# A state space model stepped by two tokens: states of odd tokens alone, even outputs by maps of their own

## Chip, cores and metric

One core of a Trainium2 chip. The metric is the device time of one launch in microseconds (us): the median of several runs, lower is better. The kernel before takes 2031.93 us.

## The reference

The program is a three-branch layer with a mixture of experts, followed by two layers of another kind; one batch, 256 tokens, width 1024, float32 throughout. The change touches the first branch, a diagonal state space model of 32 groups with 16 channels and 64 complex states each:

```python
def s5_branch(u, lam_re, lam_im, log_dt, b_re, b_im, c_re, c_im, d_skip, w_glu):
    uf = u.astype(F32).reshape(bsz, seq, SSM_GROUPS, SSM_GROUP)
    lam_bar = jnp.exp(lam * dt)
    b_bar = ((lam_bar - 1.0) / lam)[..., None] * b
    bu = jnp.einsum('bsgh,gph->bsgp', uf.astype(jnp.complex64), b_bar)
    _, states = lax.associative_scan(_ssm_combine, (a, bu), axis=1)   # s_t = lam_bar * s_(t-1) + bu_t
    y = jnp.real(jnp.einsum('bsgp,ghp->bsgh', states, c))
    y = y + d_skip * uf
    y = jax.nn.gelu(y)
    y = y * jax.nn.sigmoid(y @ w_glu)
```

Beside it run a sparse attention over 64 chosen keys (8 heads, with an index score that chooses them) and an attention over a memory of 256 rows (4 heads). Gates merge the three, an output projection adds them to x, and the experts and the two further layers follow.

## The kernel before

Activations lie as 128 channels (partitions) by 256 tokens. Dense weights come in units of 1 MB, two **pieces** of 128x1024 each (`slot`, two buffers). ScalarE (ACT) rounds a piece (`parts`, L223), VectorE (DVE) subtracts to get the rest (`parts`, L224), and TensorE (PE) multiplies in three passes (L232 to L234), 24 passes of 256 columns a piece. Three buffers of `parts` let ACT and DVE be three pieces ahead of PE. For one projection the tokens are the stationary side (L1210, 12 passes of 512 columns a piece).

The state space model stands in `class Ssm`. Set-up makes the decay and the maps `bl` (input to state, real and imaginary) by DVE and by transposes on PE (L545). For each of 16 pairs of groups (four chunks `c` of four, `j`) `chunk` does this: two float32 products of 32 rows by 128 columns over 256 tokens into one bank `ss` (L580); two multiplications on DVE by tables of cosine and sine (L587, L588), which turn the state's frame so that its decay is real; two additions on GpSimd (POOL; L589, L590); two scans along the tokens on DVE (L593); a multiplication back on DVE (L597) and one on POOL (L598); four float32 products of 128 rows by 32 columns over 256 tokens, all into the same 32 rows of the chunk's bank `yb` (L600). One float32 matmul shows in the profile as two records. `gelu` then ends a chunk. Banks of PSUM: two `dn`, four `at`, two `ss`. The two attentions (`attend`) run between chunks 0, 1, 2 and 3, and gate projections fill in.

The scheduler of the framework writes the order of the instructions on each engine when the program is built; at run time an engine takes them in that order and stops at the first that has to wait. The experts (`moe`) load 192 units of 1 MB in the order of SP's queue; the first nine (`ahead`) are issued one behind each of the last nine units of this layer's dense weights.

Of the kernel before, what the change touches and what calls it, by code (L numbers as in the profile page):

```python
# [8 lines left out]
F32 = mybir.dt.float32  # L9
# [136 lines left out]
class Ctx:  # L146
# [352 lines left out]

class Ssm:  # L500


    def __init__(self, K, pool, V):
        self.K, self.pool, self.V = K, pool, V
        nc = K.nc
        S = Small(K, pool, [128, 16], "s16", 28)
        ec = pool.tile([128, 16], F32, name="ec")
        nc.vector.memset(ec, math.e)
        dt, r = S.t(), pool.tile([128, 16], F32, name="decay")
# [4 lines left out]
        nc.vector.tensor_scalar(turn, th, 1 / (2 * math.pi), None, op0=OP.mult)  # L514
        nc.gpsimd.tensor_tensor(r, ec, lr, op=OP.pow)
        self.r = r
        sn, cs = sincos(S, K, th)
        a = S.ts(S.tt(r, cs, OP.mult), -1.0, OP.add)
        b = S.tt(r, sn, OP.mult)
        den = S.t()  # L520
        nc.vector.reciprocal(den, S.tt(S.tt(V["lre"], V["lre"], OP.mult), S.tt(V["lim"], V["lim"], OP.mult), OP.add))
        fr = S.tt(S.tt(S.tt(a, V["lre"], OP.mult), S.tt(b, V["lim"], OP.mult), OP.add), den, OP.mult)
        fi = S.tt(S.tt(S.tt(b, V["lre"], OP.mult), S.tt(a, V["lim"], OP.mult), OP.subtract), den, OP.mult)
# [3 lines left out]
        cd = pool.tile([128, 3, 16, 32], F32, name="cd")  # L527
        nc.scalar.dma_start(cd[:, :2], K.d["ssmc"])
        nc.scalar.mul(cd[:, 2], cd[:, 1], -1.0)
        self.cd = cd  # L530

        self.bl = []
        W = Small(K, pool, [128, 16, 16], "s1", K.n["s1"])
        frb, fib = (t[:, :, None].to_broadcast([128, 16, 16]) for t in (fr, fi))
        for n, (x, y, op) in enumerate(((frb, fib, OP.subtract), (fib, frb, OP.add))):
            p = W.tt(bc[:, 0], x, OP.mult)
            q = W.tt(bc[:, 1], y, OP.mult)
            bd = pool.tile([128, 16, 32], F32, name="bd", tag="s2", bufs=K.n["s2"])
            nc.gpsimd.memset(bd, 0.0)
            for g in range(2):  # L540
                s = slice(64 * g, 64 * g + 64)
                nc.vector.tensor_tensor(bd[s, :, 16 * g:16 * g + 16], p[s], q[s], op=op)
            bk = K.bank("ss")
            for c in range(4):
                nc.tensor.transpose(bk[:, c * 128:(c + 1) * 128],  # L545
                                    bd[:, 4 * c:4 * c + 4].rearrange("p a b -> p (a b)"), K.ident)
            bl = pool.tile([128, 4, 128], F32, name=f"bl{n}")
            nc.vector.tensor_copy(bl.rearrange("p a b -> p (a b)"), bk)
            self.bl.append(bl)
# [3 lines left out]
    def tables(self, c):  # L553

        K, pool, nc, turn = self.K, self.pool, self.K.nc, self.turn
        if self.tt is None:
            self.tt = pool.tile([128, T], F32, name="iota_t")
            nc.gpsimd.iota(self.tt, pattern=[[1, T]], base=0, channel_multiplier=0,
                           allow_small_or_imprecise_dtypes=True)
        tt = self.tt  # L560
        sn = pool.tile([128, 4, T], F32, name="sn", tag="tab", bufs=K.n["tab"])
        cs = pool.tile([128, 4, T], F32, name="cs", tag="tab", bufs=K.n["tab"])
        nc.gpsimd.tensor_tensor(sn, tt[:, None, :].to_broadcast([128, 4, T]),
                                turn[:, 4 * c:4 * c + 4, None].to_broadcast([128, 4, T]), op=OP.mult)
# [7 lines left out]
    def chunk(self, u, c, yb):  # L572

        K, pool, nc = self.K, self.pool, self.K.nc
        for j in range(4):
            i = 4 * c + j
            p = slice(32 * j, 32 * j + 32)
            bk = K.bank("ss")
            for n in range(2):
                nc.tensor.matmul(bk[:, n * T:(n + 1) * T], self.bl[n][p, c], u[p, c], start=n == 0, stop=True,  # L580
                                 skip_group_check=True)
# [1189 lines left out]
```

## Time and profile before

| what | value |
|---|---|
| three runs | 2032.91, 2031.72, 2031.93 us, median 2031.93 us |
| the profiled execution | 2030.49 us, its span 2028.5 us |
| share of the span, PE / DVE / ACT / POOL | 92% / 60% / 40% / 7% |
| mean granted clock of PE | 0.955 |

The span runs from the first to the last instruction; 2.0 us of the execution lie around it. A PE record lasts longer than it holds the engine, since records overlap: the time of one is read from one start to the next. The same holds, by some 0.08 us, on DVE.

### The profile page before, as it was taken

The numbers are of one execution on the slowest core, as the hardware profiler recorded it, in microseconds if no ns is written. First come the engines' busy times: TensorE is split into PE (matmuls) and PEld (weight loads), VectorE is DVE, ScalarE is ACT, GpSimd is POOL, SyncE is SP. The second block draws the span as 40 slices with busy tenths as digits, with TensorE's granted clock in tenths as the row PEclk, the third lists the DMA queues.
The fourth block names the chain that finished last, engine by engine and source line by source line (L and its number), as shares of the span: only waits on it lengthen the run. The fifth ranks groups of instructions, "written<-read, shape, count | busy, mean of one in ns | idle before, by whom it ended". The sixth has DMA issues, their size and how long they took to land.

```text
span 2028.5 us, 33538 instructions
## 1 busy us (share of the span) xinstructions
PE 1857.4 (92%) x14114; PEld 1506.7 (74%) x14114; DVE 1219.7 (60%) x1967; ACT 814.5 (40%) x1273; POOL 147.1 (7%) x110
## 2 busy tenths in 40 slices
PE   7999997876767678999999999999999899999999
PEld 6877896322212224999889998998999888998998
DVE  7898773111101104777597677777877687667775
ACT  6455542000000003544455545444544365445543
POOL 4254201000000001000100000000000100001000
PEclk9999998888887888999999999999999999999999
DMA  5422287999999998655334455554655333455553
GB/s 201 146 98 90 84 332 287 421 421 421 421 421 421 421 421 318 208 188 188 121 127 142 150 188 210 188 186 146 209 185 191 135 130 126 158 176 208 207 184 108
DMA packets 64139, 455.51 MB, mean 225 GB/s; under 512 B 7553, under 2 KB 7841, under 8 KB 9201
## 3 DMA queue, kind: packets, MB, share of 16 engines
q1 hardware_dynamic: 62960, 451.56, 59.7%
q8 instruction: 112, 1.84, 0.4%
q10 hardware_dynamic: 864, 1.41, 0.2%
q0 software_dynamic: 160, 0.35, 0.0%
q14 instruction: 43, 0.34, 0.0%
HBM read 452.25 MB, written 1.05 MB: 223 GB/s over the span
## 4 chain that ended last, share of the span: by engine, by line
PE 55%; DMA 21%; DVE 4%; ACT 2%; issue 1%; SPq 0%; DVEq 0%; ACTq 0%
DMA ahead<-wmoe 9%; PE bk_dn L241 7%; PE bk_ss L241 7%; PE bk_dn L232 5%; PE bk_dn L233 5%; PE bk_dn L234 5%; DMA parts<-wmoe 4%; PE bk_at L233 4%; DMA mraw<-wmoe 4%; PE bk_at L234 4%; PE bk_at L232 4%; PE bk_ss L242 4%; PE bk_dn L242 4%; DMA slot<-wmoe 3%; DVE parts L224 2%; PE bk_dn L1210 2%
## 5 line engine op out<-in xcount | busy, mean ns | idle before, releaser
L224 DVE TENSOR_TENSOR parts<-slot,parts 128x1024 fp32r<-128x1024 f32 x468 | 585.2, 1259 | 197.0 <-ACT parts L223 194.6
L223 ACT CAST parts<-slot 128x1024 fp32r<-128x1024 f32 x468 | 485.5, 1051 | 393.1 <-PE bk_dn L234 183.0
L234 PE MATMUL bk_dn<-hp,parts 128*128 128x256 f32 x976 | 283.0, 290 | 3.2 <-DVE parts L224 3.2
L233 PE MATMUL bk_dn<-hp,parts 128*128 128x256 f32 x976 | 281.6, 289 | 4.3 <-DVE hp L285 4.3
L232 PE MATMUL bk_dn<-hp,parts 128*128 128x256 f32 x976 | 281.1, 288 | 4.0 <-DVE kb L1375 1.8
L241 PE MATMUL bk_dn<-hp,parts 128*128 128x512 f32 x704 | 252.0, 394 | 2.4 <-DVE hp L285 2.4
L241 PE MATMUL bk_ss<-hp,parts 128*128 128x512 f32 x704 | 251.3, 393 | 0.0
L242 PE MATMUL bk_ss<-hp,parts 128*128 128x256 f32 x704 | 198.6, 282 | 0.3 <-DVE parts L224 0.3
L242 PE MATMUL bk_dn<-hp,parts 128*128 128x256 f32 x704 | 198.1, 282 | 0.0
L234 PEld LDWEIGHTS bk_dn<-hp,parts 128*128 128x128 f32 x976 | 188.9, 194 | 11.7 <-issue 6.9
L232 PEld LDWEIGHTS bk_dn<-hp,parts 128*128 128x128 f32 x976 | 188.8, 194 | 11.3 <-issue 6.7
L233 PEld LDWEIGHTS bk_dn<-hp,parts 128*128 128x128 f32 x976 | 188.7, 194 | 10.9 <-DVE hp L285 5.6
L233 PE MATMUL bk_at<-hidp,parts 128*128 128x256 f32 x704 | 195.4, 282 | 0.4
L234 PE MATMUL bk_at<-hidp,parts 128*128 128x256 f32 x704 | 194.9, 282 | 0.0
L232 PE MATMUL bk_at<-hidp,parts 128*128 128x256 f32 x704 | 186.6, 283 | 2.3 <-DVE hidp L350 2.1
L241 PEld LDWEIGHTS bk_dn<-hp,parts 128*128 128x128 f32 x704 | 132.3, 189 | 29.1 <-issue 3.4
L241 PEld LDWEIGHTS bk_ss<-hp,parts 128*128 128x128 f32 x704 | 132.3, 188 | 28.8 <-ACT parts L223 0.8
L1081 DVE TENSOR_TENSOR mhid<-ms,bk_dn 128x512 f32<-128x512 f32 x8 | 5.5, 688 | 223.2 <-PE bk_dn L1074 223.2
L242 PEld LDWEIGHTS bk_dn<-hp,parts 128*128 128x128 f32 x704 | 133.2, 189 | 3.0 <-issue 1.6
L242 PEld LDWEIGHTS bk_ss<-hp,parts 128*128 128x128 f32 x704 | 133.1, 189 | 2.1 <-DVE parts L224 0.6
L233 PEld LDWEIGHTS bk_at<-hidp,parts 128*128 128x128 f32 x704 | 133.6, 190 | 1.0 <-DVE hidp L351 1.0
L232 PEld LDWEIGHTS bk_at<-hidp,parts 128*128 128x128 f32 x704 | 128.8, 190 | 6.8 <-issue 3.0
(437 smaller groups left out, 2975.7 us busy)
## 6 DMA issues: line engine op xcount, KB each, us to landing
slot<-wdense SPq DMA_DIRECT2D x235, 1024.0 KB, 4.9
ahead<-wmoe SPq DMA_DIRECT2D x99, 1024.0 KB, 19.8
mraw<-wmoe SPq DMA_DIRECT2D x40, 1024.0 KB, 19.8
parts<-wmoe SPq DMA_DIRECT2D x31, 1024.0 KB, 19.8
slot<-wmoe SPq DMA_DIRECT2D x22, 1024.0 KB, 19.8
x<-xt SPq DMA_DIRECT2D x2, 512.0 KB, 5.5
memt<-memt SPq DMA_DIRECT2D x1, 1024.0 KB, 12.4
out<-x SPq DMA_DIRECT2D x4, 256.0 KB, 2.5
```

The costliest lines, as they stand in the source:

```text
L223: nc.scalar.copy(hi, raw)
L224: nc.vector.tensor_sub(lo, raw, hi.bitcast(F32))
L232: nc.tensor.matmul(out, whi[:, wsl], h.part(0, k), start=first, stop=False, **kw)
L233: nc.tensor.matmul(out, whi[:, wsl], h.part(1, k), start=False, stop=False, **kw)
L234: nc.tensor.matmul(out, wlo[:, wsl], h.part(0, k), start=False, stop=last, **kw)
L241: nc.tensor.matmul(bank, whi[:, wsl], h.both(k).rearrange("p a t -> p (a t)"), start=first, stop=False, **kw)
L242: nc.tensor.matmul(half(bank, 0), wlo[:, wsl], h.part(0, k), start=False, stop=last, **kw)
L1081: nc.vector.tensor_mul(hid, s, hb[1])
L1210: nc.tensor.matmul(bks[t], h.part(hp, k, slice(t * 128, t * 128 + 128)), w[wp][:, i * 512:(i + 1) * 512], start=k == 0 and n == 0, stop=k ...
```

## The change

The recurrence is stepped by two tokens. With tokens split into even (e) and odd (o), the state at an odd token is `lam_bar^2` times the state at the odd token before, plus a map (`bl[0]`, with `lam_bar` folded in) of the even input and a map (`bl[1]`) of the odd input: 128 states a row in place of 256, so the tables, multiplications, scans and additions are half as long. The output at an odd token comes from its state by the old map (`cd`); the output at an even token comes from the state of the odd token before it by a map with `lam_bar` folded in (`ce`, 127 columns), plus a direct product of its input (`direct`, 128x128). Tokens of a chunk lie apart, even ones first, from `u` (written with the two halves apart) to the last multiplication of `gelu` (which puts them in order again).

Two pairs of groups are done at once: their input products go alternately to two `ss` banks from different rows of the array (`chain`), and the sixteen output products of a chunk go in turn to four different columns of 32 (`together`), all at the chunk's end, into a bank `at`. Set-up makes two more maps `bl`, `direct` (32 products of 32x32) and `ce`. The copies of `bl` and those of `pt` in `attend` that DVE did go to ACT.

```diff
+    def chain(self, issues):
+        m = issues[0]()
+        for f in issues[1:]:
+            with self.tc.issue_after(m.ins):
+                m = f()
...
-        nc.vector.tensor_scalar(turn, th, 1 / (2 * math.pi), None, op0=OP.mult)
+        nc.vector.tensor_scalar(turn, th, 1 / (2 * math.pi), 2.0, op0=OP.mult, op1=OP.mult)
...
+        self.r = pool.tile([128, 16], F32, name="decay")
+        nc.vector.tensor_mul(self.r, r, r)
...
+        gr = S.tt(S.tt(ar, fr, OP.mult), S.tt(ai, fi, OP.mult), OP.subtract)
+        gi = S.tt(S.tt(ar, fi, OP.mult), S.tt(ai, fr, OP.mult), OP.add)
...
+        for m, (x, y) in enumerate(((gr, gi), (fr, fi))):
...
+                bl = pool.tile([128, 4, 128], F32, name=f"bl{m}{n}")
+                nc.scalar.copy(bl.rearrange("p a b -> p (a b)"), bk)
...
+        bk = K.bank("ss")
+        for n in range(2):
+            for i in range(16):
+                p, o = slice(32 * (i % 4), 32 * (i % 4) + 32), n * 128 + i // 4 * 32
+                nc.tensor.matmul(bk[p, o:o + 32], bds[n][:, i], cd[:, n, i], start=n == 0 and i < 4, stop=True,
+                                 skip_group_check=True)
...
+            nc.vector.tensor_sub(self.direct[p, :, 32 * j:32 * j + 32], bk[p, :128].rearrange("p (c m) -> p c m", c=4),
+                                 im[p])
...
+        for n, (x, y, op) in enumerate(((ar, ai, OP.subtract), (ai, ar, OP.add))):
+            t = s2("cm")
+            nc.vector.tensor_mul(ce[:, n], cd[:, 0], x)
+            nc.vector.tensor_mul(t, cd[:, 1], y)
+            nc.vector.tensor_tensor(ce[:, n], ce[:, n], t, op=op)
...
+        hs = []
+        for j in (0, 2):
+            bks = [K.bank("ss") for _ in range(2)]
+            K.chain([into(bk, j + i, n, a) for a in range(2) for n in range(2) for i, bk in enumerate(bks)])
+            h, m = (pool.tile([128, 2, 2, H], F32, name=n, tag="s2", bufs=K.n["s2"]) for n in ("sh", "sm2"))
+            cs, sn = (t[c][:, j:j + 2, None, :].to_broadcast([128, 2, 2, H]) for t in (self.cs, self.sn))
+            for i, bk in enumerate(bks):
+                v = bk[:, :T].rearrange("p (n t) -> p n t", n=2)
+                nc.vector.tensor_mul(h[:, i], v, cs[:, i])
+                nc.vector.tensor_mul(m[:, i], v, sn[:, i])
+            nc.gpsimd.tensor_tensor(h[:, :, 0], h[:, :, 0], m[:, :, 1], op=OP.subtract)
+            nc.gpsimd.tensor_tensor(h[:, :, 1], h[:, :, 1], m[:, :, 0], op=OP.add)
+            for i in range(2):
+                for n in range(2):
+                    nc.vector.tensor_tensor_scan(m[:, i, n], self.r[:, 4 * c + j + i:4 * c + j + i + 1]
+                                                 .to_broadcast([128, H]), h[:, i, n], 0.0, OP.mult, OP.add)
+            for i in range(2):
+                nc.vector.tensor_mul(h[:, i], m[:, i], cs[:, i])
+                nc.gpsimd.tensor_tensor(m[:, i], m[:, i], sn[:, i], op=OP.mult)
+            nc.gpsimd.tensor_tensor(h[:, :, 0], h[:, :, 0], m[:, :, 1], op=OP.add)
+            nc.gpsimd.tensor_tensor(h[:, :, 1], m[:, :, 0], h[:, :, 1], op=OP.subtract)
+            hs += [h[:, 0], h[:, 1]]
+        yb = half(K.bank("at"), 0)
+        nc.tensor.matmul(yb[:, :H], self.direct[:, c], u[:, c, :H], start=True, stop=False, skip_group_check=True)
...
+        K.together([out(j, n, a) for a in (1, 0) for n in range(2) for j in range(4)])
...
+        nc.vector.tensor_mul(g.rearrange("p (k a) -> p a k", a=2), apart(th), apart(y))
...
-        (nc.scalar.copy if i % 4 else nc.vector.tensor_copy)(flat(pt), bk)
+        nc.scalar.copy(flat(pt), bk)
...
+            for i in range(w):
+                nc.vector.tensor_mul(u[:, c + i].rearrange("p (a k) -> p k a", a=2),
+                                     ps[:, i].rearrange("p (k a) -> p k a", a=2),
+                                     N.rb.rearrange("p (k a) -> p k a", a=2))
```

What this does to the order of the instructions is shown at three places; rows of the change have its own line numbers (L625 are the input products, L652 the direct one, L656 the output products, L637 and L638 the multiplications after the input products, L643 the scans, L646 the multiplication back, L231 the subtraction of `parts`, L239 to L241 the passes).

PE before, in chunk 0, among the passes with the tokens stationary (L1210): the four output products of one pair of groups, then the two input products of a later one.

```order
L1210 MATMUL bk_dn<-parts,hp 128x512 x12
L600 MATMUL bk_ss<-p_1055,cd 32x256 x2
L600 MATMUL bk_ss<-p_1056,cd 32x256 x2
L580 MATMUL bk_ss<-u,bl_857 128x256
L580 MATMUL bk_ss<-u,bl_872 128x256
L1210 MATMUL bk_dn<-parts,hp 128x512 x8
```

PE now, 32 passes behind the last of those passes: all outputs of chunk 0.

```order
L848 MATMUL bk_at<-cbase,rs_r 128x128 x8
L652 MATMUL bk_at<-u,direct 128x128
L656 MATMUL bk_at<-sh,ce 32x127
L656 MATMUL bk_at<-sh,cd 32x128 x8
L656 MATMUL bk_at<-sh,ce 32x127 x7
```

What stood in sixteen places of the program as groups of four products of 256 columns stands in four places as groups of seventeen products of 128.

PE now, a little later (chunk 1, its second two pairs of groups; ten passes stand behind these rows and ahead of the next).

```order
L625 MATMUL bk_ss<-u,bl_872 128x128 x2
L625 MATMUL bk_ss<-u,bl_887 128x128 x2
L625 MATMUL bk_ss<-u,bl_902 128x128 x2
L625 MATMUL bk_ss<-u,bl_917 128x128 x2
L239 MATMUL bk_dn<-hp,parts 128x256
```

PE, what follows: the next group of input products (chunk 2), which writes the same two `ss` banks, begins right behind the first scores of the attention; one pass is put inside it.

```order
L81 MATMUL bk_at<-sq,cbase 32x256 x4
L880 LDWEIGHTS identb
L880 MATMUL bk_at<-madd_617,identb 128x512
L880 LDWEIGHTS identb
L880 MATMUL bk_at<-madd_617,identb 128x512
L885 MATMUL bk_at<-kr,qr 128x256 x4
L240 MATMUL bk_dn<-hp,parts 128x256
L241 MATMUL bk_dn<-hp,parts 128x256
L625 MATMUL bk_ss<-u,bl_872 128x128
```

DVE now, what empties the two banks between these two groups: the four multiplications stand between the subtractions of the 26th and the 27th piece.

```order
L231 TENSOR_TENSOR parts<-slot,parts 128x1024
L824 TENSOR_SCALAR madd_617<-ca 128x256
L453 TENSOR_TENSOR sm<-sm 128x256
L822 SCALAR_TENSOR_TENSOR ca<-isc,ca 128x256
L637 TENSOR_TENSOR sh<-bk_ss,cs 128x256
L824 TENSOR_SCALAR madd_620<-ca 128x256
L638 TENSOR_TENSOR sm_1568<-bk_ss,sn 128x256
L637 TENSOR_TENSOR sh<-bk_ss,cs 128x256
L638 TENSOR_TENSOR sm_1568<-bk_ss,sn 128x256
L231 TENSOR_TENSOR parts<-slot,parts 128x1024
```

Before, a group of input products took one `ss` bank and the other held `yb`; now a group takes both.

DVE before, between the subtractions of the 15th and the 16th piece:

```order
L224 TENSOR_TENSOR parts<-slot,parts 128x1024
L754 MATCH_REPLACE isc<-m_566,isc 128x256
L1243 TENSOR_TENSOR rt<-qg,cos_327 128x512
L746 TENSOR_TENSOR isc<-isc,ca 128x256
L1243 TENSOR_TENSOR rt<-qg,cos_327 128x512
L1244 TENSOR_TENSOR qr<-bk_at,sin_328 128x512 x2
L747 TENSOR_TENSOR isc<-isc,pen 128x256
L224 TENSOR_TENSOR parts<-slot,parts 128x1024
```

DVE now, the last twelve rows of the same place; 23 more rows stand between the subtraction of the 15th piece and these (four subtractions of `direct`, the index scores, four multiplications L637 and L638, three of the query's rotation).

```order
L809 TENSOR_SCALAR ca<-ca 128x256
L819 MAX m_568<-isc 128x8
L102 SCALAR_TENSOR_TENSOR rs_ms<-bk_at,nr_137 128x16
L643 SCALAR_TENSOR_TENSOR sm_1148<-decay,sh 128x128 x4
L1308 TENSOR_TENSOR qr<-bk_at,sin_330 128x512
L1309 TENSOR_TENSOR qr<-rt,qr 128x512
L804 SCALAR_TENSOR_TENSOR isc<-rel,wi,isc 128x256
L811 TENSOR_SCALAR pen<-ca 128x256
L820 MATCH_REPLACE isc<-m_568,isc 128x256
L104 TENSOR_SCALAR rs_ms<-rs_ms 128x16
L646 TENSOR_TENSOR sh<-sm_1148,cs 128x256
L231 TENSOR_TENSOR parts<-slot,parts 128x1024
```

Work that stood on both sides of several subtractions now stands between two of them.

## Rows read from the trace of the kernel before

**Rows 1.** Windows: length, PE, PEld, DVE, ACT, POOL busy (count), clock, DMA share, GB/s.

```profile
64.00:117.00 53.00, 53.00 (x351) 44.02 (x350) 52.59 (x119) 22.33 (x31) 15.78 (x11) 1.00 0.40 128
142.00:200.00 58.00, 57.93 (x385) 42.70 (x382) 47.77 (x71) 28.91 (x51) 26.64 (x21) 1.00 0.23 77
```

**Rows 2.** Waits between 75 and 265 us: total, times, longest.

```profile
ACT parts L223 <- PE bk_dn L234: 28.4, 15, 4.6
```

**Rows 3.** Groups of instructions by line, 25 to 265 us (busy, mean ns).

```profile
L224 DVE TENSOR_TENSOR parts<-slot,parts 128x1024 fp32r<-128x1024 f32 x50 | 67.8, 1356 | 12.0 <-ACT parts L223 11.8
L600 PE MATMUL bk_ss<-p,cd 128*32 128x256 f32 x128 | 31.9, 383 | 0.1
L593 DVE TENSOR_TENSOR_SCAN st<-decay,m 128x256 f32<-128x256 f32 x32 | 25.3, 816 | 7.0 <-PE bk_ss L600 5.7 <-POOL m L589 0.8 <-POOL m L590 0.3
L580 PE MATMUL bk_ss<-u,bl 32*128 32x256 f32 x64 | 18.3, 402 | 0.0
```

**Rows 4.** Timeline of PE at 120 to 124 us (start, duration).

```profile
120.24 0.64 PE L81 MATMUL bk_at<-sq,cbase 128*32 128x256 f32 x8
...
121.34 1.13 PE L821 MATMUL bk_at<-kr,qr 64*128 64x256 f32 x8
122.41 1.13 PE L580 MATMUL bk_ss<-u,bl 32*128 32x256 f32 x4
123.47 0.39 PE L233 MATMUL bk_dn<-hp,parts 128*128 128x256 f32 x1
123.69 0.28 PE L234 MATMUL bk_dn<-hp,parts 128*128 128x256 f32 x1
123.81 0.28 PE L232 MATMUL bk_dn<-hp,parts 128*128 128x256 f32 x1
```

**Rows 5.** Timeline of PE at 163 to 167 us.

```profile
163.52 1.10 PE L670 MATMUL bk_at<-pt,vt 128*64 128x128 f32 x16
164.55 1.91 PE L600 MATMUL bk_ss<-p,cd 128*32 128x256 f32 x8
166.39 1.13 PE L821 MATMUL bk_at<-kr,qr 64*128 64x256 f32 x6
```

**Rows 6.** Timeline of PE at 1047 us: products of 32x32 in four columns.

```profile
1047.75 1.21 PE L1327 MATMUL bk_ss<-gE 128*32 128x32 f32 x114
```

**Rows 7.** Windows at the start of the layer.

```profile
28.00:32.00 4.00, 1.52 (x7) 1.35 (x8) 4.00 (x4) 3.43 (x7) 1.81 (x1) 0.79 0.11 16
32.00:36.00 4.00, 4.00 (x20) 4.00 (x20) 3.09 (x16) 1.57 (x2) 0.00 (x0) 0.50 0.91 285
```

**Rows 8.** Timeline of DVE and POOL from 19 to 31 us.

```profile
19.71 2.51 DVE L285 SCALAR_TENSOR_TENSOR hp<-memt,v,hp 128x256 fp32r<-128x256 f32 x2
...
19.95 4.03 POOL L563 TENSOR_TENSOR sn<-iota_t,turn 128x1024 f32<-128x1024 f32 x2 [2.91 <-DVE turn L514]
...
28.09 2.80 DVE L224 TENSOR_TENSOR parts<-slot,parts 128x1024 fp32r<-128x1024 f32 x1
```

**Rows 9.** Timeline of DVE from 75 to 119 us.

```profile
75.85 1.22 DVE L224 TENSOR_TENSOR parts<-slot,parts 128x1024 fp32r<-128x1024 f32 x1
...
107.02 1.21 DVE L224 TENSOR_TENSOR parts<-slot,parts 128x1024 fp32r<-128x1024 f32 x1
108.16 0.68 DVE L588 TENSOR_TENSOR m<-bk_ss,sn 128x512 f32<-128x512 f32 x1
108.76 0.08 DVE L754 MATCH_VALUE_LOAD isc<-m,isc 128x8 f32 x1
...
117.81 1.29 DVE L224 TENSOR_TENSOR parts<-slot,parts 128x1024 fp32r<-128x1024 f32 x1 [0.61 <-ACT parts L223]
```

**Rows 10.** Window in the experts.

```profile
350.00:375.00 25.00, 23.31 (x257) 10.68 (x258) 4.16 (x10) 3.37 (x6) 0.00 (x0) 1.00 1.00 409
```

**Rows 11.** Timeline of SP's queue near the layer's end.

```profile
266.41 0.33 SPq L210 DMA_DIRECT2D slot<-wdense  x1
266.78 0.43 SPq L1047 DMA_DIRECT2D ahead<-wmoe  x1
```

More of the change, by code (lines that the diff above doesn't have):

```diff
@@ L497, in setup1 @@
     return V
+H = T // 2
 class Ssm:
@@ L529, in __init__ @@
-        nc.scalar.mul(cd[:, 2], cd[:, 1], -1.0)
-        self.cd = cd
-        self.bl = []
-        W = Small(K, pool, [128, 16, 16], "s1", K.n["s1"])
[L534 to L549, printed above, removed]
+        s2 = lambda name: pool.tile([128, 16, 32], F32, name=name, tag="s2", bufs=K.n["s2"])
@@ new lines, in __init__ @@
+        self.direct = pool.tile([128, 4, 128], F32, name="direct")
+        nc.gpsimd.memset(self.direct, 0.0)
+        for j in range(4):
+            p = slice(32 * j, 32 * j + 32)
+            nc.vector.tensor_sub(self.direct[p, :, 32 * j:32 * j + 32], bk[p, :128].rearrange("p (c m) -> p c m", c=4),
+                                 im[p])
+        ce = pool.tile([128, 2, 16, 32], F32, name="ce")
+        ar, ai = (t[:, :, None].to_broadcast([128, 16, 32]) for t in (ar, ai))
+        for n, (x, y, op) in enumerate(((ar, ai, OP.subtract), (ai, ar, OP.add))):
[3 more added lines that the diff above has]
+            nc.vector.tensor_tensor(ce[:, n], ce[:, n], t, op=op)
@@ L570, in tables, with chunk @@
         self.cs[c], self.sn[c] = cs, sn
[L572 removed]
+    def chunk(self, u, c):
         K, pool, nc = self.K, self.pool, self.K.nc
[L575 to L581, printed above, removed]
[L582 to L600 removed]
@@ new lines, in chunk, with into @@
+        p = [slice(32 * j, 32 * j + 32) for j in range(4)]
+        def into(bk, j, n, a):
+            return lambda: nc.tensor.matmul(bk[:, n * H:(n + 1) * H], self.bl[a][n][p[j], c],
+                                            u[p[j], c, a * H:(a + 1) * H], start=n == 0 and a == 0, stop=a == 1,
+                                            skip_group_check=True)
+        hs = []
[20 more added lines that the diff above has]
+            hs += [h[:, 0], h[:, 1]]
@@ new lines, in chunk, with out @@
+        yb = half(K.bank("at"), 0)
+        nc.tensor.matmul(yb[:, :H], self.direct[:, c], u[:, c, :H], start=True, stop=False, skip_group_check=True)
+        def out(j, n, a):
+            o, k = (yb[p[j], H:], H) if a else (yb[p[j], 1:H], H - 1)
+            return lambda: nc.tensor.matmul(o, self.cd[a][:, n, 4 * c + j], hs[j][:, n, :k], start=False, stop=n == 1,
+                                            skip_group_check=True)
+        K.together([out(j, n, a) for a in (1, 0) for n in range(2) for j in range(4)])
@@ L789, in state_space @@
         def state_space(c):
-            yb = K.bank("ss")
             if c > 1:
                 ssm.tables(c)
-            ssm.chunk(u, c, half(yb, 0))
-            ssm.gelu(u, c, half(yb, 0), g[:, c])
+            ssm.gelu(u, c, ssm.chunk(u, c), g[:, c])
         state_space(0)
```

77 lines of the change are left out of this document (41 added, 36 removed).

## The prediction

> **What bounds the kernel now.** I read the windows of the layer first, then the waits, then the groups, then single stretches of the timelines. From 64 to 117 us PE is busy all 53.00 us, at a granted clock of 1.00, the higher of its two levels (2.4 GHz); DVE is busy 52.59 of them; from 142 to 200 us PE is still full, DVE 47.77 of 58 [rows 1]. The largest wait is ACT's, 28.4 us in 15 times, for PE to give back a buffer of `parts` [rows 2]: the rounding runs ahead of the multiplying, so PE sets the pace. But up to 117 us DVE has almost nothing to spare: what is cheaper on PE alone is not gained as a whole there. That is the question of this case.
>
> PE's prices. A pass takes 0.12 us from start to start (123.69 to 123.81), and 0.22 right after a float32 product (123.47 to 123.69) [rows 4]. Two input products (four records) hold PE 1.06 us, from 122.41 to 123.47 [rows 4]; 64 records of that line were kept in the groups [rows 3], so all 32 products hold it 16 × 1.06 = 17.0 us. Four output products (eight records) take 164.55 to 166.39 = 1.84 us [rows 5]; 128 records [rows 3], 16 × 1.84 = 29.4. Together 46.4 us: what the change can work on.
>
> **The change, part by part.**
>
> *Input products.* 16 groups of two with 256 columns become 8 groups of eight with 128 columns: as many columns, but neighbours use different 32 rows and different banks. The nearest row is L821, whose products take turns between two groups of 64 rows: eight records of 256 columns in 1.07 us (121.34 to 122.41), where four records of L580 took 1.06 [rows 4]. So two ways overlap there fully. A new group has as many columns as those eight records: 1.07 us, in all 8.5 in place of 17.0, **−8.5**. Other bound: no overlap, 0. I take −8.5, because L821 differs only in the height of its row groups.
>
> *Output products.* 64 of 256 columns become 64 of 128: half the columns, 14.7 us if nothing else changed. Besides, they rotate over four column groups. L81 does so: eight records of 256 columns take 120.24 to 120.81 = 0.57 us, 0.07 each [rows 4], against 1.84/8 = 0.23 each in L600 [rows 5]. A chunk's 32 records of 128 columns are 16 such: 1.15. The direct product (two records of 128 columns, full array) I put at 0.3: half of 0.46 and the change of form. Four chunks: 4 × 1.45 = 5.8, **−23.6**. Other bound: the overlap of two column groups only, as in L670, 16 records of 128 columns in 163.52 to 164.55 = 1.03 us [rows 5]; 4 × (2.06 + 0.3) = 9.4, −20.0.
>
> *Set-up on PE.* Eight more transposes of 128 columns at half of 0.23, and 32 products of 32x32 (64 records; 114 such take 1.21 us [rows 6], so 0.7): **+1.6**.
>
> *Passes inside groups.* In the order of the change the scheduler has put passes inside five of the eight groups of input products (the third and fourth order fences show the end of one and the start of the next). Each then ends and starts the float32 form once more; after such a product a pass took 0.1 longer [rows 4], and the overlap of the two halves is lost. At 0.3 each **+1.4**. The Trainium skill, "TensorEngine Tiling (Array Packing)", Key Properties, says that a change of tiling mode drains TensorE, while tiles of one mode run independently. The 0.22 against 0.12 agrees with the first, L81 with the second.
>
> *Set-up on DVE, ACT and POOL.* Now POOL's table multiplication takes 4.03 us from 19.95, and beside it two subtractions on DVE take 2.51 us; the subtraction at 28.09 takes 2.80, where the mean is 1.356 [rows 3, 8]. PE is busy 1.52 of 4 us there and falls to a clock of 0.50 (the lower level, 1.2 GHz) right after [rows 7]. With tables half as long and, by the order of DVE, the multiplication behind `u`, I expect 2 us less before PE is full. Bounds: 0, and −6 (the idle 2.5 us of that stretch, and the 3 to 4 us that half a clock costs over 32 to 36 us and a little beyond). **−2**.
>
> The Trainium skill, "SBUF — State Buffer", says that GpSimd and a DVE instruction with two SBUF inputs take one shared pair of ports by turns, each for a whole instruction. The 2.80 beside POOL's multiplication is what that would look like; here it moves nothing else, since POOL's total work halves.
>
> *DVE.* The scans, multiplications and tables halve; the copies of `pt` and `bl` that DVE did go to ACT, which has some 30 us of idle time in each window [rows 1]. These are covered. But the work of one pair of groups is now that of two, done at once, and it meets the two subtractions between which PE must not run dry:
>
> (a) Between the subtractions of the 15th and 16th piece there are now 35 instructions (five of 512 columns at 0.60, the length of L588 from 108.16 to 108.76 [rows 9]; some 22 of 256 at about 0.33, my estimate from half that plus a fixed part; eight of 128 or fewer, 3 us in all): 13.3 us; before, seven instructions, 3.4. PE's store: three buffers, hence 72 passes at 0.12 = 8.7 us, and between them eight groups of float32 products, 6.8 us by the prices of rows 4 to 6: 15.5 us from the last pass of the 12th piece. In that time DVE and ACT must round and subtract the 15th (2.2), do the 13.3, subtract the 16th (1.2), and lose a tenth of this to POOL, 1.5 (the mean subtraction takes 1.356, that at 75.85 took 1.22 [rows 3, 9]): 18.2. **+3**.
>
> (b) The input products of chunk 2 need both `ss` banks. These are empty after four multiplications ahead of the 27th piece's subtraction (last order fence). DVE's work from the 16th subtraction to there adds up to 37 us by the same prices, before to 37.6, and before it lasted from 77.07 (75.85 + 1.22) to 119.10 = 42.0 us [rows 9]; so 40 now. PE's work on the same stretch (132 passes at 0.12 are 15.9, 48 passes of twice the columns 11.6, three input groups 3.2, an output group 1.45, other products 3.8) is 36. PE waits **+4**, in front of passes that are ready: the products stand ahead of them in its queue. The Trainium skill, "TensorEngine Tiling (Array Packing)", Gotcha 1, says that different row tiles write different banks and cannot use one bank at once; two banks a group is the price of the overlap above, and with two `ss` banks there is none to work ahead in.
>
> Behind the 27th piece DVE has 55 us of work to PE's 81, and PE is the bound again. Both stalls hang on DVE's few per cent, hence bounds: 0, and +20 (by the same prices the order puts 9 us more of DVE's work ahead of the 27th subtraction than before, 100 in place of 91; all of these and as much again, should the shorter instructions cost what the long ones do). I take +7, by the sums above.
>
> *What it becomes behind the layer.* The loads `ahead` stand in SP's queue one behind each of the last dense units (266.41, 266.78) [rows 11]; these wait for slots, so they move with PE. Later, in the experts, the DMA share is 1.00 at 409 GB/s [rows 10], and this stretch starts with those loads. Its length is fixed, so it moves by what the layer gained.
>
> **Sum:** −8.5 − 23.6 + 1.6 + 1.4 − 2 + 7 = −24.1 against the profiled 2030.5 us, 2006.4. The median stands 1.4 above it: **2008**.
>
> **Rivals.**
> - *The row groups don't overlap, or the columns only by two.* For it: the new products are of 32 rows, and no row of the trace shows these in turns. Against: L821 and L81. PE's gain falls from 30.5 to 18.4, the stalls to 5: −13.6, **2018**.
> - *DVE bounds up to 117 us.* For it: 52.59 of 53 [rows 1], and 9 us more work for it up to there. Stalls of 20 in place of 7: **2021**. Against: about half of these 9 us fall before 64 us, where DVE still has idle time.
> - *No stalls, and the early gain is larger.* With 0 and −2 to −6: −31 to −35, **1997 to 2001**. For it: DVE's sums are upper ones, since records overlap by 0.08.
> - *Nothing is passed on*: the experts' loads run as before, because their DMA and not PE sets the end. **2032**. Against: `ahead` stands behind the dense loads.
> - *Slower:* in each of eight places PE stops until the chain of the group before (multiplications on DVE, additions on POOL, scans, back) has freed banks and buffers. A chain is some 6 us of single instructions; PE's gain of 33 is used up at 4.1 us a place. At 5.5 a place, +44: **2043**. Against: between two groups the order leaves 8 us of other products or more at four of seven places.
>
> **How the numbers follow.** Likeliest 0.48 (its own range 2001 to 2014); poor overlap 0.14; DVE 0.17; no stalls 0.13; nothing passed on 0.03; slower 0.05. A measurement of this kernel tells about 0.2%, 4 us, from no change: faster 0.92, same 0.03, slower 0.05. The range 1997 to 2022 leaves out the last two, the far half of the DVE case and the best end, together under 0.2.
>
> **What would show it.** Right: an input group of 16 records in about 1.07 us, an output group with its direct product in 1.45; PE idle nowhere but twice, in front of the 16th piece's first pass and of chunk 2's first input products, 3 to 4 us each; the clock at 1.00 through it; the first `ahead` loads and the end earlier by the same 24 us. Wrong: single records at their old distances (first rival); many idle stretches of PE ended by DVE before 120 us (second), or by POOL at the groups (slower); `ahead` earlier and the end not (nothing passed on).

## The result

The changed kernel takes 2012.00 us (median of four runs, 2010.66 to 2012.83); the kernel before took 2032.42 us beside it (2031.72 to 2034.89). The ratio is 0.990, its 95% interval 0.988 to 0.991: 20 us faster. Forecast were 2008 us, with a range of 1997 to 2022. The profiled execution took 2011.24 us, its span 2009.2 us.

### The profile page after: what moved, and what is told of

Its sections match the earlier page's. It is cut to its first block, busy times and chain, and to the rows that moved or that the text cites. A ratio compares the mean times of both kernels' runs of the same rounds, so it can differ in the third digit from the quotient of the medians.

```text
span 2009.2 us, 33842 instructions
## 1 busy us (share of the span) xinstructions
PE 1822.9 (91%) x14258; PEld 1495.0 (74%) x14258; DVE 1193.5 (59%) x1986; ACT 810.4 (40%) x1281; POOL 138.5 (7%) x113
## 4 chain that ended last, share of the span: by engine, by line
PE 56%; DMA 22%; DVE 4%; ACT 1%; issue 1%; DVEq 0%; SPq 0%; ACTq 0%
DMA ahead<-wmoe 9%; PE bk_dn L248 7%; PE bk_ss L248 7%; PE bk_dn L239 5%; PE bk_dn L241 5%; PE bk_dn L240 5%; DMA parts<-wmoe 5%; DMA mraw<-wmoe 4%; PE bk_at L240 4%; PE bk_at L241 4%; PE bk_at L239 4%; PE bk_dn L249 4%; PE bk_ss L249 4%; DMA slot<-wmoe 3%; PE bk_dn L1274 2%; DVE parts L231 2%
## 5 line engine op out<-in xcount | busy, mean ns | idle before, releaser
L231 DVE TENSOR_TENSOR parts<-slot,parts 128x1024 fp32r<-128x1024 f32 x468 | 579.2, 1247 | 194.6 <-ACT parts L230 192.7
L239 PE MATMUL bk_dn<-hp,parts 128*128 128x256 f32 x976 | 280.9, 288 | 7.4 <-ACT parts L230 3.4
L241 PE MATMUL bk_dn<-hp,parts 128*128 128x256 f32 x976 | 280.1, 287 | 2.1 <-DVE parts L231 2.1
L239 PEld LDWEIGHTS bk_dn<-hp,parts 128*128 128x128 f32 x976 | 187.3, 192 | 15.0 <-issue 6.8
L241 PE MATMUL bk_at<-hidp,parts 128*128 128x256 f32 x704 | 195.0, 282 | 0.0
L241 PEld LDWEIGHTS bk_dn<-hp,parts 128*128 128x128 f32 x976 | 187.2, 192 | 5.5 <-DVE parts L231 3.3
L239 PE MATMUL bk_at<-hidp,parts 128*128 128x256 f32 x704 | 186.7, 282 | 2.4 <-DVE hidp L357 2.1
L239 PEld LDWEIGHTS bk_at<-hidp,parts 128*128 128x128 f32 x704 | 129.0, 190 | 6.6 <-issue 3.0
## 6 DMA issues: line engine op xcount, KB each, us to landing
out<-x SPq DMA_DIRECT2D x4, 256.0 KB, 2.5
```

What stands on the lines that cost most here:

```text
L231: nc.vector.tensor_sub(lo, raw, hi.bitcast(F32))
L239: nc.tensor.matmul(out, whi[:, wsl], h.part(0, k), start=first, stop=False, **kw)
L241: nc.tensor.matmul(out, wlo[:, wsl], h.part(0, k), start=False, stop=last, **kw)
```

## The profile after

**Where the layer ends.** SP's queue, start and duration of an issue, at the end of the layer's loads; the kernel before first, then the changed one.

```profile
306.59 0.33 SPq L210 DMA_DIRECT2D slot<-wdense  x1
306.96 0.43 SPq L1047 DMA_DIRECT2D ahead<-wmoe  x1
309.28 0.33 SPq L1047 DMA_DIRECT2D slot<-wmoe  x1
```

```profile
283.65 0.33 SPq L217 DMA_DIRECT2D slot<-wdense  x1
284.03 0.43 SPq L1111 DMA_DIRECT2D ahead<-wmoe  x1
286.35 0.33 SPq L1111 DMA_DIRECT2D slot<-wmoe  x1
```

The first load of `slot` for the experts comes 22.9 us earlier. Of these, 19.3 are left at the end of the span. In what follows I call this load the end of the layer: it shows the layer's own time without what comes behind it.

**PE up to there, as a sum.** Windows of the kernel before and of the changed one from 13 us to the end of the layer (columns as in [rows 1]):

```profile
13.00:64.00 51.00, 47.72 (x333) 44.09 (x334) 43.29 (x97) 31.63 (x47) 13.02 (x8) 0.93 0.45 164
64.00:309.28 245.28, 243.55 (x1720) 202.31 (x1719) 207.26 (x340) 122.64 (x202) 74.12 (x57) 1.00 0.42 148
sum 296.28, PE 291.27 PEld 246.39 DVE 250.55 ACT 154.27 POOL 87.14; mean PE 145.64 PEld 123.20 DVE 125.27 ACT 77.14 POOL 43.57
```

```profile
13.00:64.00 51.00, 49.43 (x427) 45.59 (x428) 49.18 (x126) 30.80 (x52) 15.73 (x8) 1.00 0.48 172
64.00:117.00 53.00, 46.97 (x356) 39.72 (x353) 50.09 (x128) 22.38 (x33) 27.68 (x21) 0.97 0.32 114
117.00:142.00 25.00, 23.63 (x198) 19.55 (x197) 21.66 (x47) 15.32 (x28) 15.52 (x14) 1.00 0.25 86
142.00:200.00 58.00, 55.47 (x501) 49.85 (x500) 40.91 (x78) 33.87 (x67) 18.70 (x21) 0.97 0.32 110
...
sum 273.35, PE 259.91 PEld 237.79 DVE 224.80 ACT 149.91 POOL 82.39; mean PE 43.32 PEld 39.63 DVE 37.47 ACT 24.99 POOL 13.73
```

A stretch divides into three. PE's idle time is its length less PE's busy time. What the clock takes is the missing part of the granted clock, summed here over windows of 1 us. The rest is work at the full clock.

| stretch from 13 us to the end of the layer | length | idle | taken by the clock | work |
|---|---|---|---|---|
| before | 296.3 | 5.0 | 3.4 | 287.9 |
| changed | 273.4 | 13.4 | 3.4 | 256.5 |

Work fell by 31.4 us, idle time rose by 8.4. Between 64 and 117 us, where PE was busy all 53.00 us [rows 1], it now stands still for 6 us; the waits behind that follow below.

**The new products.** PE's timeline (start, duration) around a group of input products and around one of output products:

```profile
80.06 0.28 PE L240 MATMUL bk_dn<-hp,parts 128*128 128x256 f32 x1
80.27 1.16 PE L625 MATMUL bk_ss<-u,bl 32*128 32x128 f32 x16
81.36 0.39 PE L241 MATMUL bk_dn<-hp,parts 128*128 128x256 f32 x1
...
212.22 0.39 PE L652 MATMUL bk_at<-u,direct 128*128 128x128 f32 x2
212.54 0.30 PE L656 MATMUL bk_at<-sh,ce 128*32 128x127 f32 x1
...
213.12 0.50 PE L656 MATMUL bk_at<-sh,ce 128*32 128x127 f32 x11
213.55 0.48 PE L903 MATMUL bk_at<-kmg,qmg 128*128 128x256 f32 x1
```

An input group holds PE for 1.09 us (80.27 to 81.36), forecast 1.07; so it is in the three of the eight groups that nothing else breaks up. An output group with its direct product holds PE for 1.33 (212.22 to 213.55) in two of the four chunks and for 1.54 in the other two, forecast 1.45. The rows of before are in [rows 4, 5].

**The new waits.** PE's waits from 24 to 286 us: total, times, longest.

```profile
PE bk_dn L239 <- ACT parts L230: 2.8, 3, 2.1
PE bk_ss L625 <- DVE sm L638: 2.0, 1, 2.0
PE bk_at L724 <- ACT P L720: 1.8, 2, 1.4
PE bk_dn L239 <- ACT vm L1278: 1.6, 1, 1.6
PE bk_at L1315 <- ACT qg L1297: 1.4, 1, 1.4
PE bk_dn L239 <- DVE u L925: 1.3, 1, 1.3
```

No wait is longer than 2.1 us, and no one instruction stands behind them all. Three of them can be followed back through several engines to POOL. First the one in front of input products, near 89 us; POOL (the kernel before, then the changed one), DVE and PE:

```profile
80.31 2.90 POOL L106 TENSOR_TENSOR rs_r<-rs_ms,cbase 128x16 f32<-128x16 f32 x1 [28.28 <-DVE rs_ms L104]
```

```profile
79.45 8.03 POOL L106 TENSOR_TENSOR rs_r<-rs_ms,cbase 128x16 f32<-128x16 f32 x1 [6.11 <-DVE rs_ms L104]
```

```profile
82.03 2.35 DVE L231 TENSOR_TENSOR parts<-slot,parts 128x1024 fp32r<-128x1024 f32 x2
84.30 0.41 DVE L813 TENSOR_TENSOR isc<-isc,pen 128x256 f32<-128x256 f32 x1
87.52 0.69 DVE L108 TENSOR_TENSOR rs_r<-rs_r,nr 128x16 f32<-128x16 f32 x1 [2.80 <-POOL rs_r L106]
88.13 0.41 DVE L637 TENSOR_TENSOR sh<-bk_ss,cs 128x256 f32<-128x256 f32 x1
```

```profile
89.02 0.45 PE L625 MATMUL bk_ss<-u,bl 32*128 32x128 f32 x2 [1.98 <-DVE sm L638]
```

A small power on POOL takes 8.03 us, which took 2.90 in the kernel before. DVE's multiplication by its result waits 2.80 us at the head of DVE's queue; the four multiplications that empty the two `ss` banks (of which the first is shown) stand behind it, and PE's next input products behind those. Windows of 2 us show the clock after it:

```profile
90.00:92.00 2.00, 2.00 (x14) 1.65 (x11) 2.00 (x8) 0.37 (x1) 1.72 (x3) 0.75 0.00 0
92.00:94.00 2.00, 2.00 (x6) 1.52 (x6) 2.00 (x5) 0.75 (x1) 0.00 (x0) 0.50 0.00 0
94.00:96.00 2.00, 2.00 (x10) 1.58 (x9) 2.00 (x9) 1.03 (x2) 0.32 (x1) 0.90 0.00 0
```

PE is busy, but at 1.2 GHz from 91.0 to 94.4 us, which takes 1.7 us. At the next wait, at 104 us, nothing is left of that: e12 below takes the same instructions in the same order on every engine up to 137 us, has the same wait here (2.00 us) with no fall of the clock behind it, and starts the first pass behind 104 us at 104.42, the change at 104.32.

The second one is at 149 to 152 us; DVE, then ACT, then PE:

```profile
145.11 0.76 DVE L637 TENSOR_TENSOR sh<-bk_ss,cs 128x256 f32<-128x256 f32 x2 [2.23 <-POOL sh L649]
145.78 0.68 DVE L712 TENSOR_REDUCE mx<-bk_at 128x2 f32<-128x512 f32 x1
```

```profile
146.94 1.28 ACT L716 ACT_TABLE_LOAD   x1 [5.21 <-DVE mx L714]
...
150.42 1.05 ACT L230 CAST parts<-slot 128x1024 fp32r<-128x1024 f32 x1
```

```profile
151.52 0.38 PE L239 MATMUL bk_dn<-hp,parts 128*128 128x256 f32 x1 [2.08 <-ACT parts L230]
```

DVE waits for POOL to give back a buffer of the pair before; the softmax's maximum stands behind that on DVE, the exponentials behind the maximum on ACT, and the rounding of a piece, which needs none of it, behind the exponentials. PE runs out of pieces.

The third one, at 104 us, has the same shape; ACT, then PE:

```profile
103.06 0.63 ACT L612 ACTIVATE cs<-sn 128x512 f32<-128x512 f32 x1 [3.51 <-POOL sn L611]
103.60 0.67 ACT L1278 ACTIVATE vm<-bk_dn,nr 128x512 f32<-128x512 f32 x1
```

```profile
104.32 0.39 PE L239 MATMUL bk_dn<-hp,parts 128*128 128x256 f32 x1 [1.61 <-ACT vm L1278]
```

ACT's function of a table waits for POOL, and what empties the bank that PE needs stands behind it.

## The experiments

All start from the changed kernel. The table holds the median of four runs each, the end of the layer, and the division of the stretch from 13 us to there. The kernel before, run beside them, stood at 2032.4 to 2035.5 us.

Two things limit what a row tells. The layer's end, idle time, clock and work come from one profiled execution of each run, while the four executions of a run lie between 1.3 us (e9) and 7.1 us (e6) apart; and of the ratios to the kernel before, only that of e1 has an interval clear of the change's (0.988 to 0.991). Besides, no edit leaves the order of the instructions alone: PE's differs from the change's from 53 us on in e3, from 62 in e4, from 108 in e5, from 138 in e12. So a row shows an edit together with the order that the scheduler wrote for it.

| run | median us | end of layer | idle | clock | work |
|---|---|---|---|---|---|
| changed | 2012.0 | 286.35 | 13.4 | 3.4 | 256.5 |
| e1 input products bank after bank | 2004.5 | 280.13 | 6.7 | 1.7 | 258.7 |
| e2 output products column by column | 2013.3 | 287.06 | 7.9 | 5.1 | 261.1 |
| e3 small multiplication on POOL | 2013.4 | 285.80 | 8.7 | 8.5 | 255.6 |
| e4 direct map in an `at` bank | 2010.1 | 286.45 | 10.5 | 8.5 | 254.4 |
| e5 half the key rounds | 2011.6 | 286.60 | 12.7 | 5.1 | 255.7 |
| e6 without POOL's last additions | 2010.0 | 284.00 | 8.4 | 5.1 | 257.5 |
| e7 table multiplication twice | 2010.6 | 286.60 | 10.9 | 6.8 | 255.9 |
| e8 five buffers | 2010.6 | 284.57 | 10.4 | 5.1 | 256.0 |
| e9 e1 with e8 | 2012.4 | 288.46 | 10.0 | 6.8 | 258.6 |
| e10 e1 with e3 | 2009.7 | 281.25 | 7.4 | 0.0 | 260.8 |
| e11 e1 with e4 | 2014.7 | 286.61 | 9.0 | 6.8 | 257.8 |
| e12 copies of `pt` as before | 2007.6 | 282.83 | 11.4 | 1.7 | 256.8 |

**e1, the price of the input products.**

```diff
-            K.chain([into(bk, j + i, n, a) for a in range(2) for n in range(2) for i, bk in enumerate(bks)])
+            K.chain([into(bk, j + i, n, a) for i, bk in enumerate(bks) for a in range(2) for n in range(2)])
```

> The four input products of one pair of groups are issued before the four of the other, so that neighbours use the same 32 rows of the array. A group of 16 records takes 1.09 us in the changed kernel; one after another I expect 16 x 0.133 = 2.1, over eight groups +8.3 us. Theory A (PE sets the pace, its time counts in full): 2020. Theory B (up to 125 us DVE and POOL set the pace, PE's added time falls into waits it has anyway): only the last three groups count, 2015.

Both theories fell: it became faster, 2004.5 us (ratio to the kernel before 0.985, interval 0.983 to 0.987, clear of the change's). The price itself was as expected: eight records of one bank take 1.08 us, where sixteen of two banks had taken 1.09 (from PE's timeline):

```profile
89.01 1.15 PE L625 MATMUL bk_ss<-u,bl 32*128 32x128 f32 x8
90.09 0.42 PE L81 MATMUL bk_at<-sq,cbase 128*32 128x256 f32 x4
```

Where both banks follow without a break, the second runs into the first, 1.63 us in all (81.79 to 83.42). Work rose by 2.2 us, but idle time and the clock's share fell by 8.4. The scheduler wrote another order: the first bank's two multiplications stand earlier on DVE, DVE's L108 stands behind all four, so that nothing waits for POOL at 87 us, and the waits at 104 and 149 us are gone. With all of DVE's work in place, PE has no wait above 0.4 us between 70 and 235 us, and the clock is full from 73.4 us on. So it was not DVE's amount of work that made PE wait there in the change.

**e2, the price of the rotation.**

```diff
-        K.together([out(j, n, a) for a in (1, 0) for n in range(2) for j in range(4)])
+        K.together([out(j, n, a) for j in range(4) for a in (1, 0) for n in range(2)])
```

> The sixteen output products of a chunk are issued group by group, so that neighbours use the same 32 columns. They take 1.01 us a chunk in the changed kernel (without the direct product); one after another 32 records at 0.115 = 3.7, over four chunks +10.7 us. Theory A (PE sets the pace): 2022.5. Theory B (waits swallow it up to 160 us): the last two chunks count, 2017.5.

Both theories fell. The products of a chunk take 2.18 us (107.50 to 109.68 in PE's timeline) in place of 1.01, not 3.7: the first of the next column run beside the last of the one before. Over four chunks that is 4.7 us, and the work shows 4.6 more; the median is 1.3 more, since 3.9 us of idle time and clock together went.

Some 2 us of that come from a place that the edit does not touch. Up to 107 us every engine takes its instructions in the change's order. PE was late by 2.4 us at 80 us (clock low from 68.0 to 74.8), a piece came late to DVE, DVE stood still for 0.10 us at 81.8, and POOL's power took 5.42 us in place of 8.03. DVE did not wait for it, PE did not wait for the `ss` banks at 89 us, and the pass that the change starts at 104.32 started at 102.38, 1.9 us earlier. The order was the same; what had become shorter is POOL's power.

**e3, DVE's wait for POOL.**

```diff
-            nc.vector.tensor_mul(r, r, N.r.to_broadcast([128, 2, n]))
+            nc.gpsimd.tensor_tensor(r, r, N.r.to_broadcast([128, 2, n]), op=OP.mult)
```

> The small multiplication behind the power of the norms goes from DVE to POOL, so that DVE does not stand waiting for POOL in front of the four multiplications that empty the ss banks. Theory C (PE's new waits come from chains through POOL): the 2.8 us wait of DVE near 85 us and the 2.0 us wait of PE behind it go, and the clock's dip after it: 2008 to 2010. Theory D (DVE simply has too much work there): DVE is late all the same, 2012.

The power took 2.90 us there, DVE's wait for it and PE's 2.0 us behind it went, and the layer ended 0.6 us earlier. Idle time fell by 4.8 us, the clock took 5.1 more. The median gained nothing. The named wait was real, but in this order, which is another one from 53 us on, taking it away paid nothing.

**e4, the bank of the direct map.**

```diff
-        bk = K.bank("ss")
+        bk = K.bank("at")
```

> The 32 small products of the direct map go into an at bank, so that no ss bank is held until their four subtractions on DVE are done. If that bank is what the second input product waits for near 65 us (1.4 us): that wait goes, 2010.5 to 2011. If DVE's queue is what PE waits for there, the next wait (for the query, near 68 us) grows by as much: 2012.

The second case: the wait for that bank went, the next one, for the query (L1315), grew from 1.4 to 3.3 us, and the layer ended where it did (the clock took 5.1 us more).

**e5 and e6, DVE's amount of work against POOL's chains.**

```diff
-        for r in range(8):
+        for r in range(4):
```

> Left out: four of the eight rounds that choose keys (so 32 keys in place of 64); DVE loses eight maxima and eight replacements, some 0.75 us a pair, 6 us between 75 and 120 us, and nothing else loses work. Theory D (DVE's amount of work makes PE wait up to 125 us): PE's idle time and the clock's loss shrink by 4 to 6 us, the first load slot<-wmoe goes from 286.35 to 281 to 282, 2006 to 2008. Theory C (chains through POOL hold PE up): within 2 us of the change, 2010 to 2012.

```diff
-            nc.gpsimd.tensor_tensor(h[:, :, 0], h[:, :, 0], m[:, :, 1], op=OP.add)
-            nc.gpsimd.tensor_tensor(h[:, :, 1], m[:, :, 0], h[:, :, 1], op=OP.subtract)
```

> Left out: the two additions on POOL that end the turning back of the states; POOL loses sixteen instructions of 0.73 to 1.7 us, and each chain is about 1.5 to 2.4 us shorter. Theory C (chains through POOL hold PE up): PE's idle time and the clock's loss shrink by 5 us or more, first load slot<-wmoe at 281 or before, 2007 or less. Theory D (DVE's work): within 2 us of the change, 2010 to 2012.

Without half the rounds the layer ended at 286.60, 0.25 later. But all the rounds left out stand behind 101 us (the maxima of the change at 101.1 to 116.4), and up to there every engine takes its instructions in the change's order, so that the waits at 66 to 104 us had the same work of DVE ahead of them. e5 shows that DVE's amount of work from 101 to 120 us (busy 19.0 of 19.0 us in the change, 15.7 here) does not set the time, and nothing on the work before. Without POOL's additions the layer ended at 284.00, 2.35 earlier: more than theory D allows, half of what theory C asks. Neither theory is decided by these two; for DVE's amount of work e1 speaks more clearly.

**e7, the early gain.**

```diff
+        if c < 2:
+            nc.gpsimd.tensor_tensor(sn, tt[:, None, :].to_broadcast([128, 4, H]),
+                                turn[:, 4 * c:4 * c + 4, None].to_broadcast([128, 4, H]), op=OP.mult)
```

> The multiplication that begins the tables of the first two chunks runs twice on POOL, so that it takes there what tables of full length took. If the halved length gave the early gain (PE 4.2 us earlier at the sixth piece than before): 3 to 4 us of it are lost by 45 us, 2014 to 2016. If its place in the order, behind the writing of u, gave the gain: PE stands there as in the change, 2012.

PE stood 2.1 us behind the change from the seventh piece to the twelfth, half of the 4.2 us that the change had gained there. So the halved length gave about half. With the layer's end at 286.60 us nearly nothing of the loss is left (0.25): here the time lost early did not reach the end.

**e8, buffers.**

```diff
-TAGS_A = {"a2": 2, "k2": 1, "a4": 3, "m4": 3, "s1": 5, "s2": 4, "tab": 4}
+TAGS_A = {"a2": 2, "k2": 1, "a4": 3, "m4": 3, "s1": 4, "s2": 5, "tab": 4}
...
-        S = Small(K, pool, [128, 16], "s16", 32)
+        S = Small(K, pool, [128, 16], "s16", 18)
```

> Five buffers in place of four for the states' products (room comes from one buffer less for the small tiles of gelu and 14 fewer for the 16-column tiles). If DVE's waits for POOL to give back such a buffer (2.2 us at 143 us, 1.3 us elsewhere) lead to PE's waits at 149 to 152 us: these go with the clock's dip behind them, 2007 to 2009. If not: 2012, or later, where the smaller buffers cost.

DVE's wait of 2.2 us for a buffer went (one of 1.3 us a little apart remained), and PE's waits at 149 to 152 us shrank to 0.3; the layer ended 1.8 us earlier. A wait of PE of 2.7 us at the sum of squares (L81, 66 us) came, and the clock fell at 146 us behind another wait. The median's 1.4 us are within what executions differ by.

**e9, e10 and e11, is e1's gain its own or the order's?** The edits are those of e1 with e8, e3 and e4.

> Input products bank after bank as in e1, with the five buffers of e8. Theory H (a bank filled first frees its two multiplications and so the chain of DVE and POOL earlier; worth some 6 us of the layer, whatever else is changed): first load slot<-wmoe at 278 to 281, 2002 to 2006. Theory G (e1 was a lucky placing by the scheduler, any small edit loses it): 284 to 287, 2009 to 2013.

> Input products bank after bank as in e1, with the multiplication on POOL of e3. Theory H: first load slot<-wmoe at 278 to 281, 2002 to 2006. Theory G: 284 to 287, 2009 to 2013.

> Input products bank after bank as in e1, with the direct map's products in an at bank as in e4. Theory H: first load slot<-wmoe at 278 to 281, 2002 to 2006. Theory G: 284 to 287, 2009 to 2013.

Two lost it (288.46, 286.61). The third, e10, kept it in its profiled execution (281.25), which was the fastest of its four (2005.5 us); its median, 2009.7, is what theory G expects. Filling a bank first is no gain of its own that lasts. This execution of e10 is the only one profiled in which the clock stayed up through the whole stretch; its windows:

```profile
64.00:117.00 53.00, 50.59 (x422) 43.27 (x420) 51.57 (x131) 24.00 (x36) 26.46 (x24) 1.00 0.34 117
117.00:142.00 25.00, 23.55 (x185) 19.68 (x183) 19.81 (x41) 14.67 (x27) 16.82 (x16) 1.00 0.28 88
142.00:200.00 58.00, 57.94 (x533) 52.98 (x532) 42.77 (x81) 37.22 (x78) 17.41 (x18) 1.00 0.36 125
```

**e12, the copies of `pt`.**

```diff
-        nc.scalar.copy(flat(pt), bk)
+        (nc.scalar.copy if i % 4 else nc.vector.tensor_copy)(flat(pt), bk)
```

> Every fourth copy of pt goes back from ACT to DVE, as it was before (six copies of 0.6 us). If moving them to ACT costs nothing and gains nothing (the prediction's step): first load slot<-wmoe within 1.5 us of the change's 286.35, 2010 to 2014. If ACT's queue is what PE waits for behind the softmax (149 to 152 us): 1 to 3 us earlier, 2009. If DVE's queue is: 2 to 4 us later, 2015.

The layer ended 3.5 us earlier, the median is 2007.6 us (2007.28 to 2009.77; the change's fastest was 2010.66): the second case, and more than it. Up to 137 us all engines take the change's order; PE runs 1.6 us behind the change from 107 to 132 us (clock low from 105.3 to 108.7) and is level with it again at 135, where the change waits 1.4 us. The gain comes behind that. On ACT the rounding of a piece now stands in front of the exponentials of the second softmax:

```profile
143.26 1.05 ACT L230 CAST parts<-slot 128x1024 fp32r<-128x1024 f32 x1 [1.90 <-PE bk_dn L241]
144.32 1.28 ACT L1622 ACT_TABLE_LOAD   x1
```

DVE waits for POOL's buffer here as well (2.23 us at 145 us), but PE has its pieces: the waits at 149 and 152 us and the dip of the clock behind them, 4.2 us together, are gone. Whether the copies or the rest of the new order did it, this run does not separate.

## Why the prediction was right, and where it was off

**PE's own gain was right.** Forecast were −8.5 − 23.6 + 1.6 + 1.4 = −29.1 us; the work fell by 31.4. An input group came out at 1.09 us for 1.07, an output group at 1.33 or 1.54 for 1.45; both first choices of a bound held, and the rival of poor overlap is out. That the columns overlap when they take turns is shown by e2 (2.18 us without turns, 1.01 with), the rows by e1 (1.63 us for a group bank after bank, 1.09 in turns).

**The early term was undersized.** From −2 forecast, the stretch up to 64 us gives −5.1: idle time 3.3 to 1.6, the clock's share 3.4 to 0. The bound was −6. The reason named, POOL's halved tables, is half of it (e7); that the rest is the place of that work in the order was argued, not tried.

**The stalls were undersized, and for part of them the mechanism was another.** The step that failed is "I take +7, by the sums above" with its sentence "the clock at 1.00 through it". Behind 64 us idle time rose by 10.1 us and the clock took 3.4: 13.5 where 7 stood.
- Step (a) had the right amount of work: between the subtractions of the 15th and the 16th piece (64.71 to 79.62 in DVE's timeline) DVE was busy for 14.8 us, with 40 instructions where the prediction counts 35; forecast were 13.3 and a tenth for POOL, 14.6. The wait did not come there: PE had lost 2.4 us at 64 to 69 us, in front of the `ss` bank of the direct map (1.0) and behind ACT's query (1.4), and so came later for the piece.
- Step (b) put the wait for the two `ss` banks at the first input products of chunk 2. It came at those of chunk 1 (2.0 us), and for another reason: not the sum of DVE's work, but one instruction that waited for POOL in front of the four multiplications. Where POOL's power was shorter in the same order (e2), the wait did not come.
- Counting DVE's work was the wrong measure: with the same work PE had hardly a wait behind 70 us in e1. What counted in the waits that were followed back is which instruction stands in front of which in an engine's queue. The copies of `pt` on ACT I had costed at nothing because ACT has some 30 us of idle time; with six of them back on DVE, and the order that goes with it, the layer ended 3.5 us earlier (e12). In the change ACT stood idle for 5.2 us in front of the exponentials that the late rounding stood behind: its first instruction was not ready.
- The price for POOL (its "total work halves") was wrong: from 13 us to the end of the layer it is busy 82.4 us, before 87.1; the power alone lasts 5.1 us longer. The 2.80 us that the prediction puts beside POOL's multiplication stand beside its subtraction L566 (27.45 us, 2.36 long).

The misses have opposite signs and nearly cancel: −31.4 − 5.1 + 13.5 = −23.0 against −22.9 measured (the rest is rounding) and −24.1 forecast. That the layer's sum came within 1.2 us is in part luck, since its three terms were off by 2.3, 3.1 and 6.5 us. Of the rivals, DVE as the bound put the stalls at 20, as far above 13.5 as my 7 is below, but e1 speaks against its mechanism; no stalls with a larger early gain had the early gain right and the waits not; that nothing is passed on, or that eight chains are waited out, is out. Two side sums of the rivals are a little off (poor overlap comes to −14.0, not −13.6; in the slower case the products' gain is 32.1, not 33); neither moves its time by more than 1 us.

**Behind the layer** 3.6 of the 22.9 us were lost, where I had "its length is fixed". By the loads, some 1.4 go between 740 and 830 us and some 1.7 in the last layer, where PE waits in the middle of a group of small products for nothing that the profile names:

```profile
1658.95 0.61 PE L1391 MATMUL bk_ss<-qs,kb 128*32 128x32 f32 x44
1662.10 0.38 PE L1391 MATMUL bk_ss<-qs,kb 128*32 128x32 f32 x20 [2.54 <-issue]
```

e3, e4, e5, e8, e9, e11 and e12 have it too (1.6 to 2.2 us), e6 and e7 one layer earlier (2.6 and 2.1), e1, e2 and e10 not at all. In all ten the trace has a packet of 16 KB of instructions on a DMA queue that starts 2.2 to 2.4 us before PE goes on, so it looks as if PE waits for its instructions there; no run tries it. What is lost behind the layer does not hang on it: from the layer's end to the last instruction the thirteen changed kernels take 1721.6 to 1727.2 us, 1721.9 to 1723.6 of them without the wait, and the kernel before 1719.2. Why, stays open.

**What stays open** besides: why one profiled execution loses 7 us to waits and clock and another 19, and how much of that is the order's and how much the execution's. Each wait that was followed back was real, but three times (e3, e4, e7) removing or adding one left the end of the layer within 0.6 us, because another wait or the clock took its place. e1 is a better order, at 2004.5 us faster than both kernels, and e12 by its executions; whether still better ones exist wasn't tried.

## What to carry to other kernels

Price an array that is packed by the nearest row of the trace that is packed alike: here two such rows gave the new groups' times to within 10%. Where PE gains 30 us in a layer in which DVE was full, don't stop at adding up DVE's work to find the stalls: look in each in-order queue for the short instruction that waits for a third engine in front of others that are ready. Moving one such instruction is a trial and no sure gain (e3). And treat an order written by a scheduler as one sample, and a traced execution as one more: an edit of one line moved the layer's end by up to 6 us, although PE's work had grown by 2 us (e1).

## What the runs showed of the hardware

How long POOL's power on 128x16 takes depends on what DVE runs when it starts. In the kernel before and in e3, e4, e7, e8, e9 and e11 DVE then has a maximum, a replacement or an input from a bank, and the power takes 2.89 to 2.90 us. In the change DVE is in a row of eight instructions with both inputs in SBUF (L646, L231, L646, L1309, L812, L231 twice, L813), one behind the other without a pause; they end at 84.71, and POOL is done 2.77 us later (87.48), about its whole time alone. e5, e6 and e12 repeat that: 8.03 to 8.04 us, 2.77 behind the row. In e2 the same row has its pause of 0.10 us behind L812, and POOL is done 2.77 us behind that, after 5.42 us; in e10 the row is one instruction long, 3.06 us. Only e1 does not fit wholly: there POOL waits for the end of one such instruction and not of the two behind it, 3.35 us.

The Trainium skill, "SBUF — State Buffer", section "SBUF: two separate sides", says that GpSimd and a DVE instruction with two SBUF inputs share one pair of ports, an exclusive lock that whichever starts first has for its whole instruction. The rows agree that the two exclude each other, and show POOL held off through several instructions of DVE. They do not agree that POOL has the pair for its whole instruction: in e4, L1309 and L231 of DVE run at 0.69 and 1.22 us inside a power that started 0.10 us before them. No run measured this by itself.

Falls of the clock to its lower level are not tied to one wait. In the change they come behind 2.0 us at 87 to 89 (0.75 and 0.50 from 90 to 94 us) and behind 2.1 and 0.4 at 149 to 152; in e1 behind a wait of 1.4 us at 69. e12 has the change's order up to 137 us and the wait of 2.00 us at 89, and no fall there. In e2, e3, e5, e6, e7 and e8 the clock falls between 124 and 129 us, where PE was busy throughout the windows from 120 us on, in e3 to 0.82, 0.50 and 0.82 from 124 to 130, behind groups of input products and scores. Over the runs it took between 0.0 and 8.5 us of the layer, and with one order it differs from execution to execution: up to 101 us the change, e5 and e12 take the same instructions in the same order, and lose 1.7 us at 91 to 94, 1.7 us at 70 to 73 and nothing.

An output product that goes column by column took 0.136 us (2.18/16) for 128 columns, where the kernel before took 0.46 for 256 [rows 5]: half of that is 0.23. Neighbouring columns overlap where one ends and the next begins, without being issued in turns; how far into a column this reaches was not tried.
